# Sparse attention reordered: projections, attention and compressed branch interleaved, output projection token tile by token tile

## The chip, the cores and the metric

The kernel runs on one core of a Trainium2 chip. The metric is the device time of one execution in microseconds (us), the median of the runs shown. PE is TensorE, DVE VectorE, ACT ScalarE, POOL GpSimd, SP SyncE, whose queue issues the weight loads.

## The reference, cut to what matters

The program is a stack of transformer layers over 256 tokens of 1024 features; the change is in the first mixer, native sparse attention, and touches nothing of what is computed. The mixer projects the normed input to queries and to three pairs of keys and values. The first pair (`kc`, `vc`) is compressed to 15 tokens by a small MLP; the second and third serve the selected and the window branch. Sixteen query heads share four key heads.

```python
def nsa_mixer(h, w_in, w_out, q_norm, k_norm, cmp_pos, cmp_w1, cmp_w2):
    q, kc, vc, ks, vs, kw, vw, gates = jnp.split(h @ w_in, splits, axis=-1)
    q = rmsnorm(q.reshape(B, S, NSA_HKV, G, dh), q_norm).transpose(0, 2, 3, 1, 4)
    kc = rmsnorm(compress_blocks(heads(kc), cmp_pos[0], cmp_w1[0], cmp_w2[0]), k_norm[0])
    vc = compress_blocks(heads(vc), cmp_pos[1], cmp_w1[1], cmp_w2[1])
    ks, vs = rmsnorm(heads(ks), k_norm[1]), heads(vs)
    kw, vw = rmsnorm(heads(kw), k_norm[2]), heads(vw)
    o_cmp, o_sel = nsa_compressed_selected(q, kc, vc, ks, vs, slopes)
    o_win = banded_attention(q, kw, vw, slopes, NSA_WINDOW)
    g = jax.nn.sigmoid(gates.reshape(B, S, NSA_HKV, G, 3).transpose(0, 2, 3, 1, 4))
    o = g[..., 0:1] * o_cmp + g[..., 1:2] * o_sel + g[..., 2:3] * o_win
    return o.transpose(0, 3, 1, 2, 4).reshape(B, S, NSA_HQ * dh) @ w_out
```

With 256 tokens all blocks are selected, so the selected branch is causal attention over all tokens.

## The kernel before

The 256 tokens are two token tiles of 128. Every dense product is done as three products of split operands (`mm3`, L182 to L184): a weight block of 128x1024 comes by one DMA of SP's queue into a `raw` tile (four of them), ACT rounds it to `whi` (L122) and DVE subtracts to `wlo` (L123). The split blocks stand in a ring of six slots (`wp`), in the fixed order of `_plan`; `run_ahead` loads and splits a block as soon as a slot comes free, and `free(later=True)` leaves that to the block's next use. A plan entry marked "own" goes to slots beside the ring (`self.extra`).

The mixer's stage is `nsa()`. Its steps are written in an order, and a scheduler that keeps near this order, with some steps given priority (`high_priority`), fixes each engine's instruction order at build time; each engine then runs its own queue in order. The steps:

- projections (`proj_chunk`), in chunks of 512 columns, 48 products each: chunk 2 (raw keys and values of the compressed branch), 3 and 4 (keys and values of the selected and the window branch, whose keys are normed and transposed), 0 and 1 (queries, normed and transposed).
- the blocks for the compression: chunk 2's sums go by ACT to `ckv`, by PE transposes (L525) to PSUM, and by eight DVE additions (L529) into the tiles `X`.
- `compress()` ("m"): 32 products of `X` with `cw1`, which is not split (L596), then a long chain of small steps over PE, ACT and DVE that ends in 15 compressed keys and in the values `vb`.
- `attend(i, g)` ("a" i g): for token tile i and key head g four score products (L649), softmax on DVE (L479) and ACT (L482), the gates' factor (L662 on DVE, L660 on ACT), transposes (L669), their copies (L673, L671) and the products with the values (L675). A step of tile 1 has twice the keys of a step of tile 0.
- `compressed(i)` ("c" i): the compressed branch's scores (L689) and softmax (L696 to L708); `combine(i)` ("k" i): its values (L722), the sum of the branches (L723) and the split of the result into `oh`, `ol` (L724, L725).
- `out_proj`: the output projection "no" of eight blocks, 96 products, both token tiles together; `add_x` (L331) adds it to the residual `x`. The next feed-forward layer ("f2i" weights) then transposes `x`, splits it into `xh`, `xl` (L250, L251) in the space of `oh`, `ol`, and goes on.

Before, the order is: chunk 2 (its first token tile's sums first), 3, 4, 0, the gates, then

```python
NSA_ORDER = "m a00 a01 a10 a11 q c0 a02 a03 o k0 c1 a12 a13 k1"
```

where "q" is chunk 1 and "o" only names `oh`, `ol`; the output projection follows as the last step. The tables of the compressed branch's biases (`cmp_consts`) are made in this stage, after chunk 2.

Of the kernel before, what the change touches and what calls it, by code (L numbers as in the profile page):

```python
# [20 lines left out]
F32 = mybir.dt.float32  # L21
# [10 lines left out]
P = 128  # L32
# [28 lines left out]
NSA_ORDER = "m a00 a01 a10 a11 q c0 a02 a03 o k0 c1 a12 a13 k1"  # L61
# [3 lines left out]
# columns of the per-partition constants  # L65
# [19 lines left out]
class K:  # L85
# [48 lines left out]
    def free(self, n=1, later=False):  # L134
        """later: the space is taken with the next block's use only."""
# [11 lines left out]
    def banks(self, ctx, **pools):  # L147
        """Pools of single banks of PSUM."""
# [4 lines left out]
    def bank(self, pool, *shape):  # L153
        """A bank, seen as [P, *shape]."""
# [4 lines left out]
    def rsqrt(self, v, shape, tag, pool=None, e=None):  # L159
        """1/sqrt(v), v > 0, to float32's accuracy: a first guess from the bits, then Newton."""  # L160
# [44 lines left out]
    def split_T(self, src, hi, lo, i, n, gain=None, shift=None, at=0, scale=None):  # L205
        """src [P tok, n*128] -> hi, lo [P, at..at + n, tok of tile i]; gain, shift: per feature; scale: diagonal, of
        the tokens' factors."""
# [10 lines left out]
        if PAR and n == 8 and shift is None:  # L218
            # even and odd blocks in a bank each: one is split while the other is read
# [38 lines left out]
    def proj_chunk(self, name, at, by_tile=False):  # L258
        """xT[tok i]^T @ w chunk, a bank for each i; by_tile: the first token tile's sums are complete first."""
# [67 lines left out]

    def add_x(self, scale):
# [6 lines left out]
    def ffn(self, gain, win, wout, first=False):  # L335
        nc, tc = self.nc, self.tc
        with ExitStack() as ctx:
# [8 lines left out]
            if first:  # L346
                # work for the tensor engine's clock, until the data are here
# [29 lines left out]
            # the first 256 features of both halves: tokens on partitions, their factors are not needed before the sums  # L377
# [11 lines left out]
            # the tokens' factors on all partitions  # L389
# [7 lines left out]
            # the others: features on partitions  # L397
            for f in range(2, 22):
# [20 lines left out]
    def attn_consts(self):  # L419
        """Attention biases: -slope * (t - s) with the causal mask, for key tiles 128 before and at the query tile."""  # L420
# [1548 lines left out]
```

## Time and profile before

| | us |
|---|---|
| median of 3 runs | 2273.89 |
| lowest, highest | 2264.78, 2278.5 |
| span of the profiled execution | 2278.0 |
| sparse attention's stage in it | 200.2 to 391.3 |

The span is the time from the first to the last instruction of one execution; it lies 4.1 above the median of the runs and 0.5 below the highest. The stage is one of a dozen, 8% of the span. It starts with PE's transposes of `x` and ends with the last product of the output projection.

### The profile page before, as it was taken

What the parts mean: (1) busy time and instruction counts of PE and PEld (TensorE: products, weight loads), DVE (VectorE), ACT (ScalarE), POOL (GpSimd) and SP (SyncE); (2) the same over time, 40 slices, a digit from 0 to 9 for tenths busy, and PEclk for the clock granted to TensorE, in tenths of its full rate; (3) what the DMA queues carried; (4) which work ended last, traced back from release to release, by engine and by line L of the source; (5) the groups of instructions that cost most, each with busy time, mean ns of one, the idle gap of its engine ahead of it and who ended that gap; (6) DMA issues with size and microseconds to landing.
All of it is one profiled execution on the core that took longest, in us unless ns stands there. A gap on an engine that the chain in (4) does not pass through costs nothing.

```text
span 2278.0 us, 38166 instructions
## 1 busy us (share of the span) xinstructions
PE 2231.5 (98%) x15010; PEld 1945.6 (85%) x15010; DVE 1597.0 (70%) x3223; ACT 1093.1 (48%) x1709; POOL 32.8 (1%) x75
## 2 busy tenths in 40 slices
PE   8999999999999998999999999999999999999999
PEld 7997646998899775899788777999999998888887
DVE  6766666987776587766577666896867767886555
ACT  5445575544444474544445534454533334334443
POOL 1000000000000001000000000000000000000000
PEclk9999989999999997999999999999999999999999
DMA  6565424878755542455442225456554456545664
GB/s 205 188 191 183 145 78 148 296 267 263 237 188 182 180 144 79 154 181 187 137 142 87 72 65 186 158 162 194 183 165 149 150 166 190 156 155 185 192 193 151
DMA packets 107573, 383.49 MB, mean 168 GB/s; under 512 B 13440, under 2 KB 13824, under 8 KB 107392
## 3 DMA queue, kind: packets, MB, share of 16 engines
q1 hardware_dynamic: 103392, 374.39, 51.7%
q10 hardware_dynamic: 3360, 4.55, 0.6%
q8 instruction: 118, 1.93, 0.3%
q0 software_dynamic: 640, 2.11, 0.2%
q14 instruction: 63, 0.52, 0.1%
HBM read 378.89 MB, written 2.11 MB: 167 GB/s over the span
## 4 chain that ended last, share of the span: by engine, by line
PE 85%; DVE 9%; DMA 2%; ACT 1%; issue 1%; POOL 1%; SPq 0%; DVEq 0%; ACTq 0%
PE bank L182 14%; PE bank L183 14%; PE bank L184 14%; PE pout L182 5%; PE pout L184 5%; PE pout L183 5%; PE pu L182 5%; PE pu L183 5%; PE pu L184 5%; DVE wlo L123 3%; PE pw L1648 3%; PE bank L649 1%; PE bank L675 1%; PE bank L809 1%; PE bank L669 1%
## 5 line engine op out<-in xcount | busy, mean ns | idle before, releaser
L122 ACT ACTIVATE whi<-raw 128x1024 fp32r<-128x1024 f32 x654 | 690.5, 1058 | 806.4 <-PE pout L183 202.0
L123 DVE TENSOR_TENSOR wlo<-raw,whi 128x1024 fp32r<-128x1024 f32 x654 | 797.2, 1222 | 351.1 <-ACT whi L122 348.3
L182 PE MATMUL bank<-xh,whi 128*128 128x256 f32 x1392 | 397.2, 285 | 0.0
L184 PE MATMUL bank<-xl,whi 128*128 128x256 f32 x1392 | 396.4, 285 | 0.0
L183 PE MATMUL bank<-xh,wlo 128*128 128x256 f32 x1392 | 396.0, 285 | 0.0
L182 PE MATMUL pu<-xh,whi 128*128 128x256 f32 x1024 | 292.2, 285 | 1.1 <-ACT H L1606 1.1
L183 PE MATMUL pu<-xh,wlo 128*128 128x256 f32 x1024 | 289.7, 283 | 0.0
L184 PE MATMUL pu<-xl,whi 128*128 128x256 f32 x1024 | 289.6, 283 | 0.0
L182 PEld LDWEIGHTS bank<-xh,whi 128*128 128x128 f32 x1392 | 268.7, 193 | 1.2 <-issue 0.9
L183 PEld LDWEIGHTS bank<-xh,wlo 128*128 128x128 f32 x1392 | 268.7, 193 | 0.8 <-issue 0.6
L184 PEld LDWEIGHTS bank<-xl,whi 128*128 128x128 f32 x1392 | 268.5, 193 | 0.5 <-issue 0.3
L182 PE MATMUL pout<-whi,hs 128*128 128x512 f32 x512 | 201.4, 394 | 0.0
L184 PE MATMUL pout<-wlo,hs 128*128 128x512 f32 x512 | 199.4, 390 | 0.0
L183 PE MATMUL pout<-whi,hs 128*128 128x512 f32 x512 | 199.2, 389 | 0.0
L182 PEld LDWEIGHTS pu<-xh,whi 128*128 128x128 f32 x1024 | 196.9, 192 | 1.3 <-ACT H L1606 1.3
L183 PEld LDWEIGHTS pu<-xh,wlo 128*128 128x128 f32 x1024 | 196.4, 192 | 0.0
L184 PEld LDWEIGHTS pu<-xl,whi 128*128 128x128 f32 x1024 | 196.3, 192 | 0.0
L182 PE MATMUL bank<-whi,xh 128*128 128x512 f32 x352 | 144.2, 410 | 1.9 <-ACT xh L250 1.1
L183 PE MATMUL bank<-whi,xl 128*128 128x512 f32 x352 | 142.0, 403 | 1.2 <-DVE xl L251 0.8
L184 PE MATMUL bank<-wlo,xh 128*128 128x512 f32 x352 | 141.0, 402 | 0.0
L183 PE MATMUL bank<-whi,lT 128*128 128x512 f32 x352 | 138.9, 395 | 0.0
L182 PE MATMUL bank<-whi,hT 128*128 128x512 f32 x352 | 138.2, 393 | 0.0
(545 smaller groups left out, 3390.2 us busy)
## 6 DMA issues: line engine op xcount, KB each, us to landing
raw<-in_pu_dram SPq DMA_DIRECT2D x128, 512.0 KB, 3.6
raw<-in_pv_dram SPq DMA_DIRECT2D x128, 512.0 KB, 3.6
raw<-in_f1i_dram SPq DMA_DIRECT2D x88, 512.0 KB, 3.7
raw<-in_f2i_dram SPq DMA_DIRECT2D x88, 512.0 KB, 3.9
araw<-in_wada_dram SPq DMA_DIRECT2D x48, 512.0 KB, 5.3
raw<-in_f1o_dram SPq DMA_DIRECT2D x44, 512.0 KB, 3.6
raw<-in_f2o_dram SPq DMA_DIRECT2D x44, 512.0 KB, 3.8
raw<-in_wi_dram SPq DMA_DIRECT2D x28, 512.0 KB, 3.7
```

Source lines behind the costliest of these rows:

```text
L122: nc.scalar.activation(hi, raw, AF.Copy)
L123: nc.vector.tensor_tensor(lo, raw, hi.bitcast(F32), op=OP.subtract)
L182: mm(out, lh, rh, start=start, stop=False)
L183: mm(out, ll, rh, start=False, stop=False)
L184: mm(out, lh, rl, start=False, stop=stop)
L649: nc.tensor.matmul(ps[:, :n], qT[r, h // 2, t], KT[r, g, :n], start=True, stop=True)
L669: nc.tensor.transpose(pt[:, j], prob[j][:, b, kt], self.ident)
L675: nc.tensor.matmul(ot[64 * e:64 * e + 64], v[:, kt, b, 64 * g:64 * g + 64], pT[:, e::2], start=b == 0 and kt == 0, stop=b == 1 and kt == i)
L809: nc.tensor.matmul(ps[:, :n], qT[r, h, t], kT[r, h, :n], start=True, stop=True)
L1648: nc.tensor.matmul(pw[:, t], b[:, t // 4, :, t % 4], a[:, k, t // 4, :, t % 4], start=k == 0, stop=k == 1)
```

## The change

The order of the steps is new, and the projections stand in it ("p" and the chunk's number, "g" the gates, "o" and the token tile):

```diff
-NSA_ORDER = "m a00 a01 a10 a11 q c0 a02 a03 o k0 c1 a12 a13 k1"
+NSA_ORDER = "p3 p4 p0 g a00 p1 a01 p2 a02 m a03 c0 k0 a10 o0 a11 c1 a12 a13 k1 o1"
...
+    def out_tile(self, hT, lT, blocks, i, done, last):
+        pm = [self.bank(self.mm, 512) for _ in range(2)]
+        t, nf = slice(i * P, (i + 1) * P), len(blocks)
+        def part(f, half):
+            hl, o = blocks[f], half * 512
+            self.mm3(pm[half], hT[:, f, t], lT[:, f, t], hl[0][:, o:o + 512], hl[1][:, o:o + 512], f == 0, f == nf - 1)
+        by_half = BY_HALF if last else 0
+        for f in range(nf - by_half):
+            for half in range(2):
+                part(f, half)
+            if last:
+                self.free(later=f >= nf - TAIL)
+        for half in range(2):
+            for f in range(nf - by_half, nf):
+                part(f, half)
+                if half:
+                    self.free(later=LATER)
+            with self.tc.high_priority(AHEAD):
+                done(i, half, pm[half])
...
                         self.attn_consts()
+                        self.cmp_consts(self.cmpc)
...
-            self.banks(ctx, tp=2)
-            first = ctx.enter_context(ExitStack())
-            self.banks(first, mm=2, sa=2, ot=1, cm=1)
+            self.banks(ctx, tp=2, mm=2, sa=2, ot=1, cm=1)
...
+            early = ctx.enter_context(ExitStack())
+            er = early.enter_context(tc.tile_pool(name=self.name("ne"), bufs=1, reuse_waits="tile"))
...
-            pm = self.proj_chunk("ni", (2,), by_tile=True)
-            self.cmp_consts(pr)
+                pm = self.proj_chunk("ni", (2,))
...
-                pm = self.proj_chunk("ni", (3 + b,))
+                pm = self.proj_chunk("ni", (3 + b,), by_tile=b == 0)
...
                 elif what == "m":
                     compress()
+                    early.close()
+                    self.extra = pool("wpx", 2)
...
-            first.close()
-            self.banks(ctx, mm=4)
-            self.out_proj(oh, ol, "no", 8, self.add_x(1.0), 4, 4)
+                    if at[0] == 0:
+                        blocks = [self.take("no", f) for f in range(8)]
+                    self.out_tile(oh, ol, blocks, at[0], self.add_x(1.0), at[0] == 1)
...
-        rows("no", 8)
+        rows("no", 6)
+        plan.extend(("no", (f,), "own") for f in (6, 7))
```

So chunk 1 and chunk 2 are multiplied between the attention steps of token tile 0, the compression comes after three attention steps, tile 0's output projection ("o0") stands among tile 1's attention steps, and tile 1's ("o1") after the last. All eight "no" blocks are split before o0 and held till o1; two of them stand in slots made from the scratch space of the projections and the compression, once that is done with. The biases' tables are made in the first feed-forward layer.

PE, end of chunk 2. Before, its last products are followed by the transposes of `ckv` and then by products of chunk 3 (`bank_2403`):

```order
L184 MATMUL bank_2238<-wlo_2242,xh_2141 128x512
L525 MATMUL bank_2369<-ident,ckv_2367 128x128 x4
L525 MATMUL bank_2378<-ident,ckv_2376 128x128 x4
L182 MATMUL bank_2403<-whi_2247,xh_2141 128x512
L183 MATMUL bank_2403<-whi_2247,xl_2142 128x512
```

Now, at the same place, come scores of attention step a02 (L677) and the compression's first products (L624), which read `X`:

```order
L184 MATMUL bank_3009<-wlo_2846,xh_2185 128x512
L551 MATMUL bank_3068<-ident,ckv_3066 128x128 x4
L551 MATMUL bank_3077<-ident,ckv_3075 128x128 x4
L677 MATMUL bank_3107<-KT,qT 128x256
L677 MATMUL bank_3117<-KT,qT 128x256
L551 MATMUL bank_3086<-ident,ckv_3084 128x128 x4
L551 MATMUL bank_3095<-ident,ckv_3093 128x128 x4
L624 MATMUL bank_3183<-raw_2861,X_2278 60x256
L624 MATMUL bank_3183<-raw_2875,X_2279 60x256
```

What moved: the products of two projection chunks stood behind the transposes and now stand ahead of them.

DVE, the end of the compression and what o0 waits for, in the changed kernel: the compressed keys (`cd`) and values, two splits of "no" blocks (`wlo`), the softmax of c0 (`cp`, `cm`), then k0, whose `ol` o0's products read.

```order
L654 TENSOR_TENSOR cd<-ct,rsy_3293 16x512
L664 TENSOR_TENSOR vb<-bank_3314,hdiag 128x256 x2
L123 TENSOR_TENSOR wlo_3556<-raw_3553,whi_3555 128x1024
L123 TENSOR_TENSOR wlo_3562<-raw_3559,whi_3561 128x1024
L724 TENSOR_TENSOR cp_3417<-bank_3412,cbias 128x256
L726 TENSOR_REDUCE cm_3418<-cp_3417 128x16
L727 TENSOR_TENSOR cp_3417<-cp_3417,cm_3418 128x256
L729 TENSOR_REDUCE cm_3418<-cp_3417 128x16
L751 TENSOR_TENSOR opart<-bank_3434,opart 128x4x128
L753 TENSOR_TENSOR ol<-opart,oh 128x4x128
```

Before, c0's softmax stood between softmax rows of a11 and a02, and nothing followed it closely:

```order
L696 TENSOR_TENSOR cp_3443<-bank_3438,cbias 128x256
L479 ISA sc_3489,nm_3490<-bank_3483,bias 128x128
L479 ISA nm_3490 128x1
L698 TENSOR_REDUCE cm_3444<-cp_3443 128x16
L479 ISA sc_3495,nm_3496<-bank_3493,bias 128x128
L479 ISA nm_3496 128x1
L699 TENSOR_TENSOR cp_3443<-cp_3443,cm_3444 128x256
```

What moved: the compressed branch's chain now runs straight into the output projection of tile 0.

DVE, at the end of o0 in the changed kernel: the two additions to `x` stand behind a11's factors (`prob`) and ahead of a11's copies (`pT`) and a12's softmax (L504).

```order
L690 TENSOR_SCALAR prob_3620<-prob_3620,w_3662 128x256
L690 TENSOR_SCALAR prob_3621<-prob_3621,w_3662 128x256
L355 SCALAR_TENSOR_TENSOR x<-bank_3565,x 128x512
L355 SCALAR_TENSOR_TENSOR x<-bank_3566,x 128x512
L701 COPY pT_3676<-bank_3675 128x512
L701 COPY pT_3685<-bank_3684 128x512
L504 ISA sc_3762,nm_3763<-bank_3760,bias 128x256
```

Before, tile 0's additions came after all attention, among the next layer's work (`acc` is a modulation vector summed for a later block):

```order
L889 SCALAR_TENSOR_TENSOR acc_4175<-araw_4173,silu_c,acc_4175 128x1024
L331 SCALAR_TENSOR_TENSOR x<-bank_3892,x 128x512
L331 SCALAR_TENSOR_TENSOR x<-bank_3893,x 128x512
L198 TENSOR_SCALAR ms_4076<-ms_4076 128x1
L166 TENSOR_SCALAR rsg_4081<-ms_4076 128x1
```

What moved: tile 0's additions went into the middle of tile 1's attention.

## Rows read from the trace of the kernel before

**Rows 1.** The page: the span, and busy time, share and instructions of each engine.

```profile
span 2278.0 us, 38166 instructions
PE 2231.5 (98%) x15010; PEld 1945.6 (85%) x15010; DVE 1597.0 (70%) x3223; ACT 1093.1 (48%) x1709; POOL 32.8 (1%) x75
```

**Rows 2.** Busy time of each engine by stretch of the stage (from:to, length, then busy us and instructions of PE, PEld, DVE, ACT, POOL; granted clock as a share of full speed; DMA share; GB/s): chunks 2, 3, 4, 0 and gates; the compression's products; chunk 1; the remaining attention; the rest of the output projection; the start of the next layer.

```profile
200.20:262.60 62.40, 60.58 (x296) 48.33 (x295) 47.08 (x153) 32.88 (x58) 1.74 (x8) 1.00 0.36 116
262.60:286.70 24.10, 23.00 (x132) 12.95 (x131) 14.79 (x62) 17.22 (x49) 0.00 (x0) 1.00 0.66 231
286.70:310.00 23.30, 23.30 (x123) 11.84 (x122) 18.92 (x75) 18.98 (x54) 0.00 (x0) 1.00 0.39 126
310.00:371.60 61.60, 56.20 (x300) 29.06 (x298) 34.49 (x156) 36.98 (x118) 1.02 (x2) 0.81 0.12 43
371.60:391.30 19.70, 19.60 (x91) 15.95 (x89) 15.45 (x26) 11.17 (x13) 0.29 (x1) 1.00 0.71 248
391.30:400.30 9.00, 7.67 (x35) 5.82 (x36) 9.00 (x24) 5.96 (x17) 0.00 (x0) 1.00 0.79 260
sum 200.10, PE 190.35 PEld 123.96 DVE 139.73 ACT 123.19 POOL 3.04; mean PE 31.73 PEld 20.66 DVE 23.29 ACT 20.53 POOL 0.51
```

**Rows 3.** PE in order of time (start, length), 128x512 products one behind the other in the layer ahead; the second row is the 196th after the first.

```profile
149.66 0.39 PE L182 MATMUL bank<-whi,hT 128*128 128x512 f32 x1
...
194.09 0.39 PE L183 MATMUL bank<-whi,lT 128*128 128x512 f32 x1
```

**Rows 4.** The chain of work in order of time (start, us, what; a product of full precision is two instructions here): products of the compression (L596, L614), scores of tile 1 (L649: one), products with the values (L675: two steps of four), the compressed branch's values (L722: one token tile).

```profile
275.67 1.87 PE bank L596 x14
...
288.69 1.89 PE bank L614 x32
290.58 1.05 PE bank L649 x2
...
309.14 1.04 PE bank L675 x8
...
369.92 1.75 PE bank L722 x32
```

**Rows 5.** PE and DVE in order of time while the blocks `X` are made (start, length, what, idle before it and its releaser).

```profile
220.24 1.03 PE L525 MATMUL bank<-ident,ckv 128*128 128x128 f32 x8
221.09 1.11 DVE L529 TENSOR_TENSOR X<-bank,cpos 64x512 f32<-64x512 f32 x1
...
223.28 4.11 DVE L529 TENSOR_TENSOR X<-bank,cpos 64x448 f32<-64x448 f32 x4
...
224.41 0.63 PE L525 MATMUL bank<-ident,ckv 128*128 128x128 f32 x4 [0.69 <-DVE X L529]
...
226.54 0.63 PE L525 MATMUL bank<-ident,ckv 128*128 128x128 f32 x4 [0.59 <-DVE X L529]
```

**Rows 6.** DVE's groups by line and shape in 200 to 392 (count | busy us, mean ns of one | idle before, releasers).

```profile
L123 DVE TENSOR_TENSOR wlo<-raw,whi 128x1024 fp32r<-128x1024 f32 x29 | 35.3, 1221 | 3.9 <-ACT whi L122 3.4
L479 DVE CUSTOM_DVE_ANT_0 sc<-bank,bias 128x256 f32<-128x256 f32 x32 | 12.7, 412 | 9.1 <-PE bank L649 6.7 <-ACT prob L482 1.5 <-ACT oh L724 0.8
L479 DVE CUSTOM_DVE_ANT_0 sc<-bank,bias 128x128 f32<-128x128 f32 x32 | 8.1, 285 | 13.6 <-PE bank L649 13.5
L673 DVE COPY pT<-bank 128x512 f32<-128x512 f32 x12 | 7.9, 684 | 4.0 <-PE bank L669 4.0
L479 DVE DVE_READ_ACCUMULATOR2_ANT nm<- 128x1 f32 x64 | 5.2, 82 | 0.1
...
L662 DVE TENSOR_SCALAR prob<-prob,w 128x256 f32<-128x256 f32 x16 | 4.6, 345 | 0.0
L529 DVE TENSOR_TENSOR X<-bank,cpos 64x512 f32<-64x512 f32 x4 | 4.5, 1114 | 0.1
L529 DVE TENSOR_TENSOR X<-bank,cpos 64x448 f32<-64x448 f32 x4 | 3.9, 983 | 0.1
...
L662 DVE TENSOR_SCALAR prob<-prob,w 128x128 f32<-128x128 f32 x16 | 3.6, 281 | 0.0
L723 DVE TENSOR_TENSOR opart<-bank,opart 128x512 f32<-128x512 f32 x4 | 2.8, 691 | 7.0 <-PE bank L722 7.0
...
L725 DVE TENSOR_TENSOR ol<-opart,oh 128x512 fp32r<-128x512 f32 x4 | 2.7, 674 | 0.1
...
L696 DVE TENSOR_TENSOR cp<-bank,cbias 128x256 f32<-128x256 f32 x2 | 0.8, 420 | 0.0
...
L171 DVE SCALAR_TENSOR_TENSOR rst<-rst,cs 16x4 f32<-16x4 f32 x3 | 0.4, 144 | 0.0
```

**Rows 7.** Busy time by stretch, columns as in rows 2, where the granted clock falls and rises again.

```profile
330.00:340.00 10.00, 8.97 (x31) 3.69 (x30) 3.42 (x23) 4.54 (x19) 0.00 (x0) 0.50 0.00 0
340.00:350.00 10.00, 10.00 (x36) 4.50 (x35) 3.90 (x16) 5.85 (x21) 0.00 (x0) 0.54 0.00 0
350.00:360.00 10.00, 9.32 (x64) 4.82 (x64) 8.67 (x32) 7.00 (x22) 0.00 (x0) 1.00 0.01 2
```

**Rows 8.** Who waited for whom in 200 to 310 (us in total, times, longest).

```profile
DVE x L331 <- PE bank L184: 4.0, 1, 4.0
```

**Rows 9.** The loads of the "no" blocks.

```profile
DMA to landing us min/median/max: 3.6/4.2/4.8
```

**Rows 10.** PE's first product of the next layer.

```profile
391.75 0.49 PE L182 MATMUL bank<-whi,xh 128*128 128x512 f32 x1 [0.55 <-ACT xh L250]
```

More of the change, by code (lines that the diff above doesn't have):

```diff
@@ L534, in nsa, with blocks_of @@
-            for b in range(2):
-                pm = self.proj_chunk("ni", (3 + b,))
-                for i in range(2):
-                    kk = self.wk.tile([P, 4, 64], F32, name=self.name("kk"), tag="kk")
+            def blocks_of():
+                pm = self.proj_chunk("ni", (2,))
+                for i in range(2):
+                    for j in range(2):
+                        ckv = er.tile([P, 4, 2, 64], F32, name=self.name("ckv"), tag="ckv", bufs=2)
+                        nc.scalar.activation(ckv, pm[i][:, 256 * j:256 * (j + 1)].rearrange(
+                            "p (h d) -> p h d", h=4).unsqueeze(2).to_broadcast([P, 4, 2, 64]), AF.Copy, scale=rs[i])
+                        pt = self.bank(self.tp, 4, P)
+                        for h in range(4):
+                            nc.tensor.transpose(pt[:, h, :], ckv[:, h].rearrange("p a d -> p (a d)"), self.ident)
+                        for half in range(2):
+                            r = slice(64 * half, 64 * half + 64)
+                            n0, n1 = max(8 * i, half), min(8 * i + 8, 15 + half)
+                            nc.vector.tensor_tensor(
+                                X[j][r, :, :, n0 - half:n1 - half].rearrange("p l h n -> p h n l"),
+                                pt[r].rearrange("p h (n l) -> p h n l", l=16)[:, :, n0 - 8 * i:n1 - 8 * i],
+                                pos[r, j].unsqueeze(1).unsqueeze(1).to_broadcast([64, 4, n1 - n0, 16]), op=OP.add)
@@ L538, in nsa, with keys @@
+            def keys(b):
+                pm = self.proj_chunk("ni", (3 + b,), by_tile=b == 0)
+                for i in range(2):
+                    kk = er.tile([P, 4, 64], F32, name=self.name("kk"), tag="kk", bufs=2)
                     nc.scalar.activation(kk, pm[i][:, :256].rearrange("p (h d) -> p h d", h=4), AF.Copy, scale=rs[i])
@@ L727, in nsa @@
             for what in NSA_ORDER.split():
-                if what == "q":
-                    queries(1)
+                at = [int(z) for z in what[1:]]
+                if what[0] == "p":
+                    queries(*at) if at[0] < 2 else blocks_of() if at[0] == 2 else keys(at[0] - 3)
+                elif what == "g":
+                    sigmoids()
                 elif what == "m":
                     compress()
+                    early.close()
+                    self.extra = pool("wpx", 2)
                 elif what[0] == "c":
-                    compressed(int(what[1]))
+                    compressed(*at)
                 elif what[0] == "a":
-                    attend(int(what[1]), int(what[2]))
-                elif what == "o":
-                    oh = self.xp.tile([P, 8, S], F32R, name="oh", tag="xh")
-                    ol = self.xp.tile([P, 8, S], F32R, name="ol", tag="xl")
-                else:
-                    combine(int(what[1]))
-            first.close()
-            self.banks(ctx, mm=4)
-            self.out_proj(oh, ol, "no", 8, self.add_x(1.0), 4, 4)
+                    attend(*at)
+                elif what[0] == "k":
+                    if at[0] == 0:
+                        oh = self.xp.tile([P, 8, S], F32R, name="oh", tag="xh")
+                        ol = self.xp.tile([P, 8, S], F32R, name="ol", tag="xl")
+                    combine(*at)
+                else:
+                    if at[0] == 0:
+                        blocks = [self.take("no", f) for f in range(8)]
+                    self.out_tile(oh, ol, blocks, at[0], self.add_x(1.0), at[0] == 1)
+            self.extra = None
     def diff(self):
@@ L1765, in nsa @@
     def nsa():
-        proj("ni", (2, 3, 4, 0))
         for what in NSA_ORDER.split():
@@ L1769, in nsa @@
                 plan.extend(("cw1", (j, u), False) for u in range(4) for j in range(2))
-            if what == "q":
-                proj("ni", (1,))
-        rows("no", 8)
+            if what[0] == "p":
+                proj("ni", (int(what[1]),))
+        rows("no", 6)
+        plan.extend(("no", (f,), "own") for f in (6, 7))
     def diff():
@@ L1830, in _tile_kernel_body @@
                 k.ac = c3.enter_context(tc.tile_pool(name="ac", bufs=1))
-                if start < 1:
-                    k.ffn("ffn1_0", "f1i0", "f1o0", True)
-                else:
-                    k.attn_consts()
-                if stop == 1:
-                    return finish()
-                if start < 2:
-                    k.nsa()
+                with ExitStack() as c4:
+                    k.cmpc = c4.enter_context(tc.tile_pool(name="cmpc", bufs=1, side="right", reuse_waits="tile"))
+                    if start < 1:
+                        k.ffn("ffn1_0", "f1i0", "f1o0", True)
+                    else:
+                        k.attn_consts()
+                        k.cmp_consts(k.cmpc)
+                    if stop == 1:
+                        return finish()
+                    if start < 2:
+                        k.nsa()
                 if stop == 2:
```

75 lines of the change are left out of this document (30 added, 45 removed).

## Prediction

> **What bounds the kernel now.** I read the page first: PE is busy for 2231.5 of 2278.0 us, and no other engine is near that [rows 1]. The change moves work inside one stage, so the second view is the stage cut into stretches [rows 2]. PE is idle there for 1.82, 1.10, 0, 5.40 and 0.10 us, and for 1.33 in the first 9 us of the next layer: 9.75 in all. The only stretch at less than full clock is 310 to 371.6 (0.81): of its 61.6 us a share of 0.19 was lost, for as much of the time as PE was busy (56.20 of 61.6), some 10.7 us. PE's products are the same before and after, so what a new order can win is these two, about 20 us or 0.9%. That ceiling is an estimate (where products wait inside a pipeline, idle time can count as busy), but it says that a gain above 1% needs the idle time and the clock's loss to vanish together. There is no such ceiling on a loss.
>
> The stage's first four stretches show how it is covered now. While DVE builds the blocks `X` (four additions at 1.114 and four at 0.983, 8.4 us [rows 6]), PE's two short waits are 0.69 and 0.59 [rows 5], because products of chunk 3 follow. While the compression's chain of small steps runs, chunk 1's products keep PE busy for 23.30 of 23.30 us [rows 2]. So the time that dense products hide now is what the change has to hide in another way.
>
> **The change part by part**, by stretches of the new order. A product of 128x512 takes 0.227 us: 196 of them from 149.66 to 194.09 [rows 3].
>
> *Chunks 3, 4, 0, gates.* The first stretch (62.4) loses chunk 2's 48 products (10.9), its 16 transposes (8 in 1.03 [rows 5], 2.1) and its short waits (1.3): 48.1 us, between 47.5 and 50.
>
> *Chunks 1 and 2 with a00 and a01.* 96 products are 21.8, the queries' transposes some 1.8, two attention steps of tile 0 some 8.4 of PE's time (a step has eight scores' worth of pieces and two groups of four products with values, 0.52 each by the 1.04 for two steps [rows 4], and transposes and weight loads in between; an estimate). That is 32. The norm of the queries stands in DVE's queue among a01's softmax rows, and the first softmax waits for a step of ACT; I take 5 for such waits: 36.9, between 32 and 39.
>
> *From the end of chunk 2 to o0.* Here the term that decides. DVE's queue in the new order holds, priced by [rows 6]: the additions to `X`, 8.4; a02 and a03, each eight softmax rows at 0.285 + 0.082, four factors at 0.281, a copy at 0.684 and about 0.5 of small steps, 5.25 a step, 10.5; a10, the same at 0.412 and 0.345, 5.8; seven rows of a11, 3.5; eight `wlo` splits at 1.221, 9.8 (four blocks more than such a stretch needed before: the "no" blocks are now wanted all at once); the compression's own chain, about 5.5 (its steps are like the 0.144 of L171, with some at 0.4 to 0.7); c0's softmax, 2.8 (its additions at 0.420); k0, two sums at 0.691 and a split at 0.674, 2.05. Together 48.3 us. PE's work there is 32 products of the compression at 0.267 (14 instructions in 1.87 [rows 4], two to a product), 8.5, the scores of a02, a03 and a10, the transposes, and 1.89 and 1.75 for L614 and L722: about 34. So PE, which sets the time elsewhere, waits for DVE here. The first piece is visible in the order itself: `X` needs 8.4 us of DVE, and behind the transposes PE has only two scores of a02; about 5.9 us of it lie bare, where 1.3 did. On top of the 48.3 come the hops of the chain, which no wide product covers: the new order has the compression's chain, c0, L722 and k0 in one line, and each change of engine costs a piece like the 0.55 that PE waits for `xh` [rows 10]. DVE's own idle time in front of such steps was 7.0 us for four sums L723 and 13.5 for the softmax rows of tile 0 [rows 6]; I take 12 for the stretch. That is 60, between 48.2 (DVE never waits) and 68 (two thirds more waits). I lean to the middle, since six attention rows can run beside the chain but not behind it.
>
> *o0 and what lies in it.* 48 products, 10.9, and transposes and products of a10, 2.6: 13.5. DVE's queue has the two additions to `x` ahead of a11's copies and a12's softmax. It comes to them about 5.4 us after `ol` and stands till the sums are complete, some 8 us. Before, such a wait was 4.0 [rows 8], at a place where only splits stood behind it. PE has o0's products meanwhile, so the price falls due in the next stretch. [...]
>
> *The rest of a11, c1, a12, a13, k1.* PE has about 25 us of work, DVE 24, and the steps alternate with little else. Before, attention steps of about twice that number took 61.6, with a part at half clock [rows 2, 7]. I take 30, between 25 and 36.
>
> *o1.* 48 products, 10.9. Before, the whole projection stood at the end and hid the loads and splits of its own blocks and of the next layer's.
>
> The sum: 48.1 + 36.9 + 60 + 13.5 + 30 + 10.9 = 199.4, against 191.1 (200.2 to 391.3): +8.3.
>
> *Edits beside this.* The next layer's first product waits 0.55 for `xh`, the stretch idles 1.33 [rows 2, 10], and its first four blocks are now split by the end of o1: I take -1 (0 to -1.4; `xh` still goes into the space of `oh`, which o1 reads to its end). The tables for the biases move about 3.3 us of DVE into the first layer, behind products without a gap and a ring of blocks split ahead: nothing, or up to 3 if that cover is gone. The two "no" blocks outside the ring wait for the scratch space; their loads land in 3.6 to 4.8 us [rows 9] and come during the chain, and their two splits (2.45) stand ahead of c0's softmax on DVE: in the sum above.
>
> *The clock.* Before, it stood at 0.50 and 0.54 from 330 to 350, where PE had 31 and 36 instructions in 10 us, and at 1.00 from 350, where it had 64 [rows 7]. The stretch from 310 had full-speed work for about three quarters of its time and lost 10.7; the new one from chunk 2 to o0 has 34 of 60, so it will hardly hold full clock; but DVE sets the time there, and slower products cost only what DVE waits for. I take +7, between 0 and 10.7 and more (the second rival). [...]
>
> So +8.3 - 1 + 7 = +14.3 on the execution of 2278.0. That execution lies 4.1 above the median; 2292.3 times 2273.89 / 2278.0 is 2288.
>
> **The rivals.** *First, the fills do what dense products did (faster).* If attention rows fill the hops, the stretch to o0 takes DVE's bare 48, the rest 26, the clock stays full: 199.4 - 12 - 4 = 183.4, -7.7, with -1 for the next layer and up to -4 where o0 covers DVE's backlog: -12.7, about 2261. For it: before, DVE was busy for 34.49 of 61.6 us in the attention stretch [rows 2], so its waits there were long and a better mix has something to fill. Against it: the mix now has fewer dense products in the chain's neighbourhood, not more.
>
> *Second, the half clock takes over the whole chain (slower).* If from the first scores of a02 the clock stays at half until o0, PE's 34 become up to 68, PE and DVE alternate, and the stretch takes 78 instead of 60. That takes the place of most of the +7; a third of the 10.7 lost before (3.5) stays for the sparse rest. 199.4 + 18 - 191.1 = +26.3, -1 for the next layer, +3.5: +28.8, about 2302 (+1.3%). A loss above 1% begins at +22.8 on the execution, so the point from which it decides is a stretch of 72 us between chunk 2's last product and o0's first. For it: 20 us at half clock in a stretch where PE was busy for 9 of 10 us [rows 7]. Against it: o0's and chunk 2's products on either side are dense.
>
> *Third, the change doesn't do what it says:* the two blocks beside the ring come too late, since their space is free only when the compression has ended. Then o0 waits at its seventh block for up to a landing, 4.8 [rows 9], and two splits, 2.45: 2295 at most, inside the range of the forecast.
>
> **How the numbers follow.** The forecast (PE waits in the compression's chain more than it did, and what it wins back elsewhere is less: 2276 to 2297) has a chance of 0.57, the third rival in it. The first rival has 0.23, of which 0.03 is a gain above 1%; the second 0.20, of which all lies above 1%. The runs spread over 0.6%, and about 1% is what a measurement of this kernel can tell from no change. So faster 0.03, same 0.77, slower 0.20. The range for 8 in 10 goes from 2264, which leaves out the better third of the first rival, to 2306, which leaves out the worse half of the second.
>
> **What would show it.** PE idle for about 6 us between the last products of chunk 2 and the first of L624. From there to o0 about 60 us with DVE near 80% and PE near 57% busy, a granted clock under 1 in it. DVE idle for about 8 us ahead of tile 0's addition to `x` (L355). The stage's end 8 to 16 us after 391.3. No gap on PE in the first layer where the tables are made. The forecast is wrong if the stretch to o0 takes under 52 us, or if the clock is at full speed throughout.

## The result, and the profile after

The changed kernel takes 2291.64 us, the median of 4 runs (2290.87 to 2293.75); the kernel before takes 2273.32 beside it. The ratio is 1.0086, with a 95% interval from 1.0069 to 1.0104: slower, by 18 us at the medians. The forecast was 2288. The profiled execution has a span of 2290.0 and a run time of 2291.77.

The page, span and engines, which answers [rows 1]:

```profile
span 2290.0 us, 38174 instructions
PE 2232.6 (97%) x15010; PEld 1946.9 (85%) x15010; DVE 1599.5 (70%) x3223; ACT 1094.9 (48%) x1709; POOL 32.5 (1%) x75
```

Over the whole execution PE's busy time is the same within 1.1 us, so nearly all of the 12.0 us by which the spans differ is time in which PE waits. The stage in stretches, columns as in [rows 2]: chunks 3, 4, 0 and gates; chunks 1 and 2 with a00 and a01; from the end of chunk 2 to o0's first product; o0; the rest of tile 1's attention; o1; the start of the next layer.

```profile
200.20:247.06 46.86, 46.42 (x225) 37.17 (x224) 37.95 (x118) 32.34 (x56) 0.00 (x0) 1.00 0.52 165
247.06:281.63 34.57, 34.44 (x166) 23.59 (x165) 17.90 (x99) 21.64 (x60) 0.00 (x0) 1.00 0.14 46
281.63:346.36 64.73, 48.82 (x251) 25.36 (x249) 41.34 (x133) 32.89 (x95) 0.00 (x0) 0.71 0.38 130
346.36:361.36 15.00, 15.00 (x77) 10.64 (x76) 5.18 (x17) 6.00 (x19) 0.00 (x0) 1.00 0.00 1
361.36:398.04 36.68, 31.68 (x162) 16.25 (x160) 17.86 (x72) 18.26 (x52) 1.31 (x2) 0.72 0.12 44
398.04:410.21 12.17, 12.16 (x56) 9.77 (x56) 9.74 (x11) 8.43 (x9) 0.00 (x0) 1.00 0.62 212
410.21:419.50 9.29, 7.85 (x35) 5.80 (x36) 9.08 (x26) 5.08 (x15) 0.00 (x0) 1.00 0.97 362
```

The stage ends at 410.2, where it ended at 391.3: 18.9 us later. Of these, 13.1 are idle time of PE (21.5 us in the first six rows, 8.4 before) and 5.8 are busy time (products that take longer at a lower clock, as L642's 3.57 us for 1.89 below). Two stretches hold most of it, and both have a mean clock near 0.7 (the records show two levels only, 1.00 and 0.50, full and half speed): the one to o0 (64.73 us, PE idle for 15.9, DVE busy for 41.34) and the rest of the attention (36.68, PE idle for 5.0). Between them stands o0, with PE full and DVE busy for 5.18 of 15.00 us.

PE while `X` is made, which answers [rows 5]:

```profile
281.47 1.03 PE L551 MATMUL bank<-ident,ckv 128*128 128x128 f32 x8
282.44 0.70 PE L677 MATMUL bank<-KT,qT 64*128 64x256 f32 x4
284.32 0.63 PE L551 MATMUL bank<-ident,ckv 128*128 128x128 f32 x4 [1.18 <-DVE X L555]
286.42 1.08 PE L551 MATMUL bank<-ident,ckv 128*128 128x128 f32 x4 [1.47 <-DVE X L555]
288.43 1.11 PE L624 MATMUL bank<-raw,X 128*60 128x256 f32 x2 [0.93 <-DVE X L555]
290.53 1.97 PE L624 MATMUL bank<-raw,X 128*60 128x256 f32 x8 [0.99 <-DVE X L555]
```

The waits 0.69 and 0.59 have become 1.18, 1.47, 0.93 and 0.99: 4.6 us, where there were 1.3. Then PE along the end of the compression's chain, from `h` to o0 (one name in brackets for each step that PE waited for):

```profile
318.38 3.57 PE L642 MATMUL bank<-cw,h 128*15 128x64 f32 x32 [1.41 <-DVE h L637]
321.88 2.08 PE L677 MATMUL bank<-KT,qT 64*128 64x512 f32 x4
325.18 1.93 PE L677 MATMUL bank<-KT,qT 64*128 64x512 f32 x4 [1.22 <-DVE rst L171]
327.41 2.04 PE L677 MATMUL bank<-KT,qT 64*128 64x512 f32 x2 [0.30 <-DVE rsy L172]
329.38 0.61 PE L658 MATMUL bank<-ident,cd 16*128 16x16 f32 x4
330.39 1.22 PE L661 MATMUL bank<-ct,spread 16*128 16x256 f32 x2 [0.41 <-ACT KT L659]
332.62 1.08 PE L717 MATMUL bank<-qT,KT 64*32 64x256 f32 x8 [1.01 <-DVE vb L664]
...
340.47 0.66 PE L739 MATMUL bank<-ident,cp 128*128 128x128 f32 x2 [3.58 <-DVE cp L736]
341.60 3.29 PE L750 MATMUL bank<-cpT,vb 128*64 128x128 f32 x32 [0.47 <-ACT cpT L740]
...
346.36 0.48 PE L182 MATMUL bank<-whi,oh 128*128 128x512 f32 x1
```

Nearly every step of it is followed by a wait (the longest, 3.58, for c0's softmax), and products take longer than before: L642's 32 take 3.57 where the like ones took 1.89, L750's 32 take 3.29 where they took 1.75 [rows 4]. DVE at the end of o0, which answers [rows 8], and the next layer's first product, which answers [rows 10]:

```profile
360.70 1.39 DVE L355 SCALAR_TENSOR_TENSOR x<-bank,x 128x512 f32<-128x512 f32 x2 [5.86 <-PE bank L184]
```

```profile
411.42 0.47 PE L182 MATMUL bank<-whi,xh 128*128 128x512 f32 x1 [1.21 <-DVE x L355]
```

For the experiments one more measure is used: the **stage** from the first product of the first projection chunk to the next layer's first product, 203.1 us in the changed kernel and 182.5 before, and the time that the clock stood at half in it, 58.0 and 23.9 us.

### The profile page after: what moved, and what is told of

The parts are those of the page before. It is cut to its first block, busy times and chain, and to the rows that moved or that the text cites. A ratio compares the mean times of both kernels' runs of the same rounds, so it can differ in the third digit from the quotient of the medians.

```text
span 2290.0 us, 38174 instructions
## 1 busy us (share of the span) xinstructions
PE 2232.6 (97%) x15010; PEld 1946.9 (85%) x15010; DVE 1599.5 (70%) x3223; ACT 1094.9 (48%) x1709; POOL 32.5 (1%) x75
## 4 chain that ended last, share of the span: by engine, by line
PE 85%; DVE 9%; DMA 2%; ACT 2%; issue 1%; POOL 1%; SPq 0%; DVEq 0%; ACTq 0%; POOLq 0%
PE bank L182 14%; PE bank L183 14%; PE bank L184 14%; PE pout L182 5%; PE pout L184 5%; PE pout L183 5%; PE pu L182 5%; PE pu L183 5%; PE pu L184 5%; PE pw L1683 3%; DVE wlo L123 3%; PE bank L677 1%; ACT whi L122 1%; PE bank L844 1%; PE bank L703 1%
```

## The experiments

Each was timed beside the kernel before (median 2274 to 2277 in each set), with 4 to 10 runs each. The last two columns, in us, come from one profile per kernel.

| run | median us | ratio to before, 95% interval | stage | at half clock in it |
|---|---|---|---|---|
| the kernel before, as profiled first | 2273.32 | | 182.5 | 23.9 |
| before_again | 2274.14 (one run) | | 175.4 | 6.8 |
| the changed kernel | 2291.64 | 1.0086, 1.0069 to 1.0104 | 203.1 | 58.0 |
| swap | 2288.83 | 1.0064, 1.0041 to 1.0088 | 199.5 | 51.2 |
| latex | 2290.24 | 1.0069, 1.0043 to 1.0095 | 203.2 | 58.0 |
| oldorder_o | 2279.67 | 1.0027, 1.0008 to 1.0046 | 192.7 | 37.5 |
| o_last | 2284.28 | 1.0045, 1.0028 to 1.0062 | 192.1 | 37.5 |
| swap_olast | 2284.89 | 1.0051, 1.0033 to 1.0069 | 191.1 | 34.1 |
| best1 | 2274.08 | 1.0006, 0.9986 to 1.0025 | 179.4 | 10.2 |
| best3 | 2276.76 | 1.0008, 0.9991 to 1.0025 | 186.1 | 27.3 |
| nosplit | 2289.67 | 1.0063, 1.0044 to 1.0083 | 201.6 | 58.0 |
| fill2 | 2294.59 | 1.0096, 1.0061 to 1.0130 | 201.1 | 20.5 |
| fill3 | 2292.58 | 1.0071, 1.0046 to 1.0097 | 200.7 | 30.7 |
| fillE | 2296.48 | 1.0098, 1.0067 to 1.0129 | 203.2 | 44.4 |

### Which part of the order: oldorder_o, o_last, best1

```diff
-NSA_ORDER = "p3 p4 p0 g a00 p1 a01 p2 a02 m a03 c0 k0 a10 o0 a11 c1 a12 a13 k1 o1"
+NSA_ORDER = "p2 p3 p4 p0 g m a00 a01 a10 a11 p1 c0 a02 a03 k0 o0 c1 a12 a13 k1 o1"   # oldorder_o
+NSA_ORDER = "p3 p4 p0 g a00 p1 a01 p2 a02 m a03 c0 k0 a10 a11 c1 a12 a13 k1 o0 o1"   # o_last
+NSA_ORDER = "p2 p3 p4 p0 g m a00 a01 a10 a11 p1 c0 a02 a03 k0 c1 a12 a13 k1 o0 o1"   # best1
```

With chunk 2 first again, the token tile whose sums are complete first is set as before (in chunk 2, not in chunk 3).

> The order of the kernel before for projections, compression and attention, with the new output projection: o0 behind k0 among tile 1's attention steps, o1 at the end. Theory 1 (the loss comes from dense products taken away from the additions to X and from the compression's chain): the loss goes, 2270 to 2279, and o0 may keep the clock up in the attention stretch. Rival (the output projection in two parts with eight blocks held, and its wait in DVE's queue, is the loss): 2285 or more.

> The changed kernel with o0 moved behind k1, directly ahead of o1; projections and compression stay in the new order. Theory 1 (the order of the projections is the loss): it stays, 2287 to 2297, rather more than less since o0's products no longer run beside a11. Rival (o0's place is the loss): 2273 to 2280.

> The order before for projections, compression and attention, with the output projection written as o0 o1 at the end, so that the scheduler may put single products of o0 between the attention steps of tile 1 once k0 is done. Theory 3 (two causes: chunk 1 must cover the compression's chain, and o0's products must be spread, not stand in one block): faster than the order before with o0 behind k0 (2279.7): 2262 to 2272. Rival (splitting the output projection costs by itself, by the wait for ol at the end and by o1 alone): 2275 to 2283.

The old order with the new output projection gives back 12 of the 18 us (stage 10.4 shorter), o0 moved alone 7 (stage 11.0 shorter), both together 17.6 (stage 23.7 shorter); oldorder_o missed the top of the first theory's range by 0.7. Each is a cause. Their shares go by the times, since the stage of one kernel can vary by 7.1 from one execution to the next, as the kernel before shows below. best1 keeps all else of the change (the banks, the output projection in two parts with eight blocks held, the tables in the first layer) and is as fast as the kernel before, so none of this is a loss that can be told.

The first cause is the cover: in oldorder_o PE is full while the compression's chain runs, as it was before [rows 2]. Its second and third rows show the attention steps up to o0 and o0 itself:

```profile
286.00:310.00 24.00, 24.00 (x125) 12.10 (x124) 20.16 (x75) 20.03 (x57) 0.00 (x0) 1.00 0.39 133
310.00:353.52 43.52, 37.49 (x167) 18.04 (x166) 24.57 (x116) 27.05 (x89) 0.00 (x0) 0.70 0.13 46
353.52:365.40 11.88, 11.88 (x54) 9.49 (x56) 3.19 (x9) 2.23 (x5) 0.00 (x0) 0.94 0.00 1
```

The same part of the chain, from the first step of `h` on DVE to the start of `vb`, in the kernel before and then in the changed one:

```profile
281.99:304.02 22.03, 22.03 (x110) 11.80 (x109) 18.08 (x69) 18.59 (x52) 0.00 (x0) 1.00 0.56 184
311.03:331.71 20.68, 15.41 (x60) 7.11 (x60) 14.62 (x55) 14.52 (x37) 0.00 (x0) 0.65 0.45 155
```

The chain takes no longer than it did, though the mean clock is 0.65 instead of 1.00; what is gone is the work that PE did beside it, 110 instructions against 60. (Before, chunks 3, 4 and 0 follow chunk 2 and cover the making of `X`, and chunk 1 covers the chain; now all four stand ahead of chunk 2's end.) oldorder_o puts back the whole order up to o0. The run best3, told below, parts this further: it differs from o_last in having chunk 2 first (with the token tile setting above), the compression behind the gates and chunk 1 behind a01, and it takes 2276.76 us against 2284.28.

The second cause the forecast did not have. In the changed kernel 39 of o0's 48 products stand in one block, and a11's transposes (L697) behind it, although their inputs are done 5 to 6 us earlier (`prob`, by DVE here, its other half by ACT at 355.8):

```profile
353.70 1.14 DVE L690 TENSOR_SCALAR prob<-prob,w 128x256 f32<-128x256 f32 x4
```

```profile
352.14 0.50 PE L182 MATMUL bank<-whi,oh 128*128 128x512 f32 x1
...
360.96 0.40 PE L184 MATMUL bank<-wlo,oh 128*128 128x512 f32 x1
361.20 1.03 PE L697 MATMUL bank<-ident,prob 128*128 128x128 f32 x8
```

o0 is written ahead of a11 to a13, and the scheduler keeps near the written order. Written behind them, it is taken in pieces where PE would wait. In o_last, the stretch to o0, then tile 1's attention with o0's products strewn in, then the rest to the end of o1:

```profile
282.58:348.28 65.70, 49.54 (x256) 25.51 (x254) 42.05 (x134) 32.95 (x95) 0.00 (x0) 0.71 0.38 129
348.28:385.94 37.66, 37.65 (x223) 20.79 (x220) 18.45 (x72) 21.99 (x69) 1.08 (x2) 1.00 0.13 43
385.94:400.44 14.50, 14.42 (x66) 11.27 (x65) 12.54 (x21) 10.02 (x12) 0.23 (x1) 1.00 0.70 237
```

The first row is like the changed kernel's (64.73); the other two are 52.2 us, where the changed kernel needs 15.00 + 36.68 + 12.17 = 63.9. While tile 1's attention runs, PE is full and the clock whole. o_last's time (2284.28) fell below what the first theory expected of it, and its rival's range was not reached either: both causes were at work.

best1 has both mends; its stage from 310 on:

```profile
310.00:352.00 42.00, 36.06 (x197) 18.17 (x196) 29.56 (x133) 30.42 (x99) 0.00 (x0) 0.88 0.14 48
352.00:388.00 36.00, 34.19 (x193) 24.25 (x191) 23.31 (x50) 17.93 (x34) 1.31 (x2) 1.00 0.57 187
```

best1's time, 2274.08, fell between the two expectations, and is no different from the kernel before's: strewing o0's products wins nothing that can be told here once the rest is as before.

### Two mixed orders: best3, swap_olast

```diff
+NSA_ORDER = "p2 p3 p4 p0 g m a00 a01 p1 a02 a03 c0 k0 a10 a11 c1 a12 a13 k1 o0 o1"   # best3
+NSA_ORDER = "p3 p4 p0 g a00 p2 a01 p1 a02 m a03 c0 k0 a10 a11 c1 a12 a13 k1 o0 o1"   # swap_olast
```

> As the run before, but all of tile 0 ahead of tile 1 (chunk 1 behind a01, then a02, a03, c0, k0, then a10 to a13), so that o0's products are ready for nearly all attention steps of tile 1. Theory 3: more of o0 is spread, little half clock behind k0, 2258 to 2272. Rival (the chain a02, a03, c0, k0 is bare before o0 can start, as in the changed kernel): 2275 to 2288.

> The changed kernel with both single edits: chunk 1 and 2 exchanged, and o0 moved behind k1. Theory 3: the two gains add (3 and 7 us): 2279 to 2284. Rival (they are one gain, the clock's): 2284 to 2289.

best3 is also as fast as before, within its interval. Its steps up to k0, then the attention behind k0:

```profile
292.00:342.00 50.00, 42.48 (x183) 21.16 (x181) 35.07 (x148) 31.39 (x94) 0.00 (x0) 0.73 0.23 73
342.00:393.00 51.00, 50.89 (x281) 31.80 (x280) 30.52 (x93) 31.23 (x80) 1.30 (x2) 1.00 0.28 90
```

The attention behind k0 is dense, but the steps up to k0 lie at a mean clock of 0.73. The time is in the rival's range, and that stretch fits the reason that the rival gave. In swap_olast the two edits do not add: 2284.89 against 2284.28 for o_last alone, in the range of its rival. That both are one gain, the clock's, as the rival had it, is not shown: it stood at half for 34.1 us in swap_olast's stage and for 37.5 in o_last's.

### The additions to X: swap

```diff
-NSA_ORDER = "p3 p4 p0 g a00 p1 a01 p2 a02 m a03 c0 k0 a10 o0 a11 c1 a12 a13 k1 o1"
+NSA_ORDER = "p3 p4 p0 g a00 p2 a01 p1 a02 m a03 c0 k0 a10 o0 a11 c1 a12 a13 k1 o1"
```

> Only the places of chunk 1 and chunk 2 in the order are exchanged: the products of chunk 1 now stand behind those of chunk 2, so they can run while DVE makes X. Theory 1 (the additions to X lie bare: PE idle or nearly so for 6 of the 7 us from 281.6 to 288.4): the wait before L624 is gone, and the time falls by 4 to 6 us, to 2286 to 2288. Rival (the half clock in the compression's chain sets the loss): the chain behind is as sparse as it was, the time stays at 2291 within 2.

The compression's products follow chunk 1's without a wait:

```profile
284.83 0.39 PE L184 MATMUL bank<-wlo,xh 128*128 128x512 f32 x1
285.14 3.67 PE L624 MATMUL bank<-raw,X 128*60 128x256 f32 x32
289.48 0.66 PE L586 MATMUL bank<-ident,q 128*128 128x128 f32 x4 [0.67 <-DVE q L583]
290.92 0.70 PE L677 MATMUL bank<-KT,qT 64*128 64x256 f32 x2 [0.78 <-ACT qT L587]
```

Of PE's 4.6 us of waits for `X`, 1.5 are left (ahead of the transposes of `ckv`), and two new ones have come, for the queries of chunk 1 (0.67 and 0.78). The stage is 3.6 us shorter, but it also stood 6.8 us less at half clock, so how much of the 3.6 is the cover of `X` can't be told. The time is 2.8 us less, between the two expectations, and the intervals do not part it from the changed kernel's. What lay bare at `X` is read from the changed kernel's own trace: 4.6 us, not 5.9.

### DVE's queue in the stretch to o0: nosplit

```diff
...
+            if name == "no":
+                self.made.append((hi, hi))
+                continue
             nc.vector.tensor_tensor(lo, raw, hi.bitcast(F32), op=OP.subtract)
```

> The changed kernel without DVE's splits of the eight output blocks: whi is used in place of wlo, so the small parts of these weights are left out of the computation, and PE does the same number of products. It takes eight operations of 1.22 us from DVE, all between the end of chunk 2 and o0, six of them among the five small steps of the compression. Theory 1 (DVE's queue sets that stretch): o0 starts 5 to 9 us earlier after chunk 2 than the 64.7 us now, the time falls to 2283 to 2287. Rival (the hops and the half clock set it): 0 to 3 us, 2289 to 2293.

```profile
281.80:345.87 64.07, 50.31 (x250) 26.14 (x249) 32.60 (x125) 32.85 (x95) 0.00 (x0) 0.68 0.37 132
```

DVE's busy time fell from 41.34 to 32.60, the stretch from 64.73 to 64.07. The rival holds: DVE's queue alone does not set this stretch. (The clock stood at half for 41.0 us of it, 3.4 more than in the changed kernel; at the prices found below, 0.31 to 0.41 us for each, that hides some 1.1 to 1.4 us of gain, an estimate.) Where the gain went can be seen on PE. (L646 is L642 above, L681 the scores L677, L662 the transposes of `cd`, L658.)

```profile
314.47 3.57 PE L646 MATMUL bank<-cw,h 128*15 128x64 f32 x32 [1.56 <-DVE h L641]
...
319.02 5.25 PE L681 MATMUL bank<-KT,qT 64*128 64x512 f32 x6
325.67 2.04 PE L681 MATMUL bank<-KT,qT 64*128 64x512 f32 x2 [1.40 <-DVE nm L508]
327.64 0.61 PE L662 MATMUL bank<-ident,cd 16*128 16x16 f32 x4
```

The product of `h` starts 3.9 us earlier (314.47 against 318.38): the five small steps that feed it no longer stand among six splits. But the keys follow only 1.7 earlier, behind tile 1's scores at half clock, of which one waits for the softmax ahead of it, and o0 only 0.5 earlier.

### The clock: fill2, fill3, fillE, before_again

Products that nothing reads were put into the sparse stretches (`fb` is a bank of the projections that is free there; those behind steps of the chain read the step's output, so that they stand where they are meant to; in fillE they read `oh`).

```diff
+            def fill(n):
+                for _ in range(n):
+                    nc.tensor.matmul(fb[0], self.xh[:, 0, :P], self.xh[:, 0:2].rearrange("p a s -> p (a s)"), start=True, stop=True)
+            def fillg(a, n):
+                k, m = a.shape
+                for _ in range(n):
+                    nc.tensor.matmul(fb[0][:m, :256], a, v[:k, 0, 0], start=True, stop=True)
...
+                fillg(hx[:, 0, 0], 3)
```

> The changed kernel with products added that nothing reads (36 of 128x512 among the additions to X and the scores of a02, a03 and a10; 24 of 256 columns in full precision behind steps of the compression's chain and of c0), about 20 us of PE work between the end of chunk 2 and o0. Theory 2 (half clock is what makes that stretch long: 37.5 us of it at half clock, PE at 0.71): the clock is granted there, and in spite of the added work the stretch takes 64.7 us or less (56 to 65), the time 2283 to 2291. Rival (DVE's queue and the hops of the chain set it, as forecast, the clock costs little): the clock is granted but the stretch stays at 65 to 75, the time is 2291 to 2301.

> The changed kernel with fewer added products than in the run with added products before (28 of 128x512 among the additions to X and the scores of a02 and a03, 13 of 256 columns behind steps of the chain, none behind the compressed keys), so that few of them stand ahead of the chain's steps. Theory 2 (half clock is a large part of the stretch's length): the stretch to o0 takes 57 to 62 instead of 64.7, the time 2284 to 2289. Rival (the chain over DVE and ACT sets it whatever the clock): 63 to 66, 2289 to 2294.

> The changed kernel with 24 products of 128x512 that nothing reads (5.5 us of PE work) among the scores and transposes of a12 and a13, where the clock stood at half for 20.5 us. Theory 2: the clock is granted there and the stretch from o0's end to o1 falls from 36.7 to 31 to 34, the time to 2286 to 2289, although work was added. Rival (the steps' own hops set it): 36 to 39.

> The kernel before once more, for its profile: the stage from its first product of chunk 2 to the next layer's first product took 182.5 us and the part between the next layer's end and the experts 897.1, where the kernels of this study, which do the same work there, show 889 to 898. If the stage varies by less than 4 us, the difference of the stages (203.1 against 182.5) is the change's doing, and the 7 us in which the two profiles differ elsewhere are not.

The stretch to o0 and the rest of tile 1's attention, first in fill2, then in fill3:

```profile
281.72:347.57 65.85, 60.46 (x335) 35.05 (x333) 41.30 (x133) 32.41 (x95) 0.00 (x0) 0.92 0.38 129
362.57:396.10 33.53, 28.29 (x162) 14.84 (x161) 17.82 (x72) 18.17 (x52) 1.30 (x2) 0.85 0.14 49
```

```profile
281.49:345.41 63.92, 55.54 (x305) 30.80 (x303) 42.28 (x134) 32.48 (x95) 0.00 (x0) 0.87 0.40 132
360.40:394.90 34.50, 29.50 (x164) 15.57 (x161) 17.85 (x72) 18.13 (x52) 1.31 (x2) 0.80 0.14 47
```

In the stretch to o0 the clock rose from 0.71 to 0.92 and 0.87, and the length stayed: 65.85 and 63.92 against 64.73. By the lengths the rivals hold, yet these runs part the causes poorly: the added products are work on PE's path too, so a gain by the clock and a loss by the fill may cancel. What they show is that PE had room for 335 instructions (busy for 60.46 us) in the time that it took for 251 (48.82).

The rest of the attention is cleaner. In fill2 and fill3 nothing was added there, and the clock happened to stand at half for less of it: 20.5 us in the changed kernel, 13.7 in fill3, 10.2 in fill2, with lengths of 36.68, 34.50 and 33.53. So 10.2 us at half clock cost 3.15 us, or 0.31 for each. PE's idle time in it is 5.0 us in the first two and 5.2 in the third: what half clock adds there is busy time. fillE, with 24 products added in this stretch, took as long as the rival had it:

```profile
361.69:399.47 37.78, 33.83 (x187) 17.74 (x185) 18.44 (x72) 18.36 (x52) 1.30 (x2) 0.91 0.13 43
```

There 5.5 us of added work stand against 13.7 us less at half clock.

The kernel before, profiled again, gives a second price. Its stretch from 310 to 371.6, now and in [rows 2]:

```profile
310.00:371.60 61.60, 56.13 (x331) 31.52 (x328) 38.77 (x161) 42.28 (x124) 1.31 (x2) 0.94 0.18 60
```

The clock was at 0.94 there instead of 0.81, and 331 instructions of PE fit into it instead of 300. The stage is 175.4 instead of 182.5, with 17.1 us less at half clock: 0.41 us for each. Until the clock falls, the two executions run alike (in the first three rows of [rows 2] PE is now busy for 60.56, 23.07 and 23.30 us); no order of instructions explains the difference. The stage varied by 7.1, more than the 4 that the expectation allowed, so by these profiles the change costs 20.6 to 27.6 us in the stage (latex, in effect the changed kernel again, shows its 203 a second time).

### Tile 0's additions to x: latex

```diff
-NSA_ORDER = "p3 p4 p0 g a00 p1 a01 p2 a02 m a03 c0 k0 a10 o0 a11 c1 a12 a13 k1 o1"
+NSA_ORDER = "p3 p4 p0 g a00 p1 a01 p2 a02 m a03 c0 k0 a10 o0 a11 c1 a12 a13 x0 k1 o1"   # x0: tile 0's add_x
...
+                elif what == "x0":
+                    for z in late:
+                        self.add_x(1.0)(*z)
...
```

> Only tile 0's two additions to x (L355) are moved, from the end of o0 to behind a13. Theory 1 (first in, first out on DVE: it stood 5.9 us for o0's sums with a12's softmax behind): the stretch from o0 to o1 shortens by 3 to 6 us, the time falls to 2286 to 2289. Rival (that stretch is set by PE at half clock and by the hops of the steps, 375 to 395): no change, 2290 to 2293.

```profile
359.92 1.39 DVE L355 SCALAR_TENSOR_TENSOR x<-bank,x 128x512 f32<-128x512 f32 x2 [5.86 <-PE bank L184]
```

The run says nothing on its question: although written behind a13, the additions were placed at the end of o0 again, with the same wait. What the trace of the changed kernel shows is told below.

## Why the prediction was right, and where its steps were not

**The time and its sign** came out: 2291.64 in the forecast's own range of 2276 to 2297, and the stage ends 18.9 us late, where 8 to 16 were named (15.3 by the sum and the clock). That the new order lays the compression's chain bare, and so costs more than it wins, is shown. The nearness of the sum is in part luck: one term was too long, others too short, the largest was right by two errors that offset each other, and one of the two causes was not in the forecast.

**Chunks 3, 4, 0, 1 and 2** were put at 48.1 + 36.9 = 85.0 and took 46.86 + 34.57 = 81.4. The 5 us of waits in the second did not come: PE was busy for 34.44 of 34.57.

**The stretch to o0** was put at 60 and took 64.73. That a main loss comes with the cover is shown by oldorder_o and by best3 against o_last. How the 60 were made up was wrong. The forecast took DVE's queue as the base (48.3, DVE 80% busy, PE 57%) and waits as an addition (12). DVE was busy for 41.34 us there (64%, PE 75%), so 23.4 were waits. The work foreseen did come: the eight splits, and fifteen of tile 1's softmax rows (a10's eight, and seven of a11):

```profile
L504 DVE CUSTOM_DVE_ANT_0 sc<-bank,bias 128x256 f32<-128x256 f32 x15 | 6.0, 412 | 1.3 <-PE bank L677 1.3
```

But one record on DVE often begins before the one ahead of it has ended (a softmax row of 0.29 us begins at 290.51, the next record at 290.72): the durations of all groups in this view add up to some 47 us, in 41.34 of busy time. The forecast added durations. And taking 8.7 us of DVE's time away moved o0 by half a microsecond. What sets the stretch, as far as these runs show, is the chain of single steps that wait for each other over PE, DVE and ACT, with tile 1's scores in between: from the transposes of `cht` (309.97) to o0's first product 36.4 us in the changed kernel, and 35.5 in nosplit and 36.7 in fill3, where `cht` stands at 310.34 and 308.73. Of PE's 15.9 us of idle time 4.6 wait for `X` (5.9 foretold) and 3.6 for c0's softmax; the rest is spread over the chain's steps. No run shortened DVE's part and the clock's part together, so how far this chain can be pressed stays open.

**o0 and what follows** were put at 13.5 + 30 + 10.9 = 54.4 and took 63.9; the middle term's 36.68 lies above its own range of 25 to 36. The price that the forecast named was DVE's wait in front of L355. It was seen (5.86, with 8 foretold), but it held nothing back. Next on DVE are a11's copies, and their transposes stand on PE behind the same block of 39 products; the copies begin at 362.01, the first transposes at 361.20. That DVE keeps the order of its queue is seen in the trace of before: it stood 2.82 us, to 23.98, for POOL's `rsy`, and the split behind began only at 24.18, though its `whi` was done at 21.9. But what stood behind L355 could not yet run. The cost was in PE's own queue: dense products spent as a block, then a stretch without any. No rival had this mechanism, and o_last measures it: 11.7 us (63.9 against 52.2). By the changed kernel's own rows these are mostly the 5.0 us of idle time in the rest of the attention and its 20.5 us at half clock, some 6.3 at 0.31 (an estimate).

**The clock** was put at +7, "0 to 10.7 and more". The stage had 58.0 us at half clock. The 6.3 of the rest of the attention alone take up nearly all of the 7; for the 37.5 us in the stretch to o0 no price could be parted from the fill, so by how much the term was too small stays open. The mean clock was 0.71 and 0.72 in these two sparse stretches and 1.00 in o_last where products are strewn in; what grants it is not shown. The 10.7 that the forecast took for before's own loss was one execution's: the second had 6.8 us at half clock in its stage instead of 23.9.

**Nothing or less:** the next layer's first product was to come 1 us closer; its wait grew from 0.55 to 1.21, and the term fails with the wrong sign. The tables in the first layer cost nothing on PE, as forecast: it is busy for all of the time from 40 to 200 us, and the first projection starts at 208.3 us, before at 209.2. The output blocks were in time: o0 ran without a wait. The third rival is out.

**The first rival** (the fills do as meant) needed the stretch to o0 under 52 and a whole clock; neither came. **The second** needed more than 72; it reached 64.73.

**Slips in the working**, none of which changes the forecast: 32 and 5 are 37.0, not 36.9. The 5.8 for a10 leaves out its eight 0.082 (6.5 with them). Behind the 4.0 of [rows 8] stood the norm's steps, which need the same `x`, and not only splits.

The two first profiles differ by 12.0 us, though the stages differ by 20.6. Most of this lies far behind the change: from the end of the next layer to the experts, where the kernels do the same work, the profile before has 897.1 us, the one after 890.0. The clock goes with it: it stood at half for 41.0 us of that part in the one, for 30.7 in the other. In all fourteen profiles this part took 889.4 to 892.2 us where 30.7 to 34.1 were at half clock, 893.1 to 897.1 at 37.5 to 41.0, and 897.9 to 898.3 at 44.4 to 47.8. Why the clock falls for longer in one execution than in another stays open.

## What to carry to other kernels

Before moving dense products, name the chain of small steps that they cover now: here taking the dense chunks from behind such steps cost 7.5 us (best3 against o_last) to 12 us (oldorder_o against the changed kernel), and the attention steps put in their place did not cover it. With a scheduler that keeps near the written order, dense work that should fill gaps must be written behind the steps with gaps, or it is spent as one block (63.9 us against 52.2 in o_last). An engine that stands in front of a late result costs only what could have run behind it, here nothing for DVE's 5.86 us; look at where the inputs of that work stand in the other queues.

## What the runs showed of the hardware

The same kernel, executed twice, stood at half clock for 23.9 and for 6.8 us in one stage and differed there by 7.1 us: a share of the spread of its times (2264.78 to 2278.5). At half clock a sparse stretch does not take twice its time: each microsecond so spent cost 0.31 us (rest of the attention) to 0.41 us (the stage before). Over the fourteen profiles, from the end of the next layer to the experts, it is about 0.5 us (an estimate, by a line through lengths of 889.4 to 898.3 us with 30.7 to 47.8 us at half clock).
